# A two-layer transformer trunk: work moved off GpSimd, the feed-forward norm on ScalarE, other buffers for the down product's first loads

## The chip, the core and the metric

The kernel runs on one core of a Trainium2 chip. The metric is the device time of one execution in microseconds. Three runs of the kernel before gave a median of 2775.42 us (2772.57 to 2777.33). The engines are TensorE (PE, matmuls, with its weight loads as PEld), VectorE (DVE), ScalarE (ACT), GpSimd (POOL) and SyncE (SP), which issues the transfers.

## The reference, cut to what matters

The input is 1024 tokens of 1024 channels in fp32, and there are two layers. Each layer has a token mixer with two attention branches and a squared-relu feed-forward block:

```
h = rms_norm(x, mix_norm_g[l])
proj = h @ w_in[l]                      # q, k, v of both branches and two gates
o_sb  = stick_breaking_attention(...)   # branch A, 8 heads of 64
q = apply_rope(rms_norm(sw_q, q_norm_g[l]), cos, sin)
k = apply_rope(rms_norm(sw_k, k_norm_g[l]), cos, sin)
y_swa = sliding_window_sink_attention(q, k, v, sinks[l]) @ w_branch_swa[l]
merged = gates[0] * (o_sb @ w_branch_sb[l]) + gates[1] * y_swa
x = x + merged @ w_out[l]
h2 = rms_norm(x, mlp_norm_g[l])         # x * rsqrt(mean(x*x) + eps) * g
x = x + square(relu(h2 @ w_up[l])) @ w_down[l]
```

`w_up` is 1024 x 4096 and `w_down` 4096 x 1024.

## The kernel before, in words

Every fp32 product is made of three fast matmuls: each operand is split into a high part, made by an ACT cast, and a low part, a DVE subtract of the high part from the source (L332 and L335 for the mixer's weights, L1266 and L1269 for the feed-forward part). `three` (L346 to L348) issues high·high, high·low and low·high. So each weight tile passes DMA, ACT and DVE before PE can use it.

The order of the instructions is fixed when the program is built. A model of the machine, `Plan`, runs processes that ask for an engine ("A" ACT, "D" DVE, "G" GpSimd, "P" PE, "S" SP) with a cost and a rank, and each engine's queue gets its instructions in the order in which the model grants them. Each engine works its queue in that order, so an instruction that waits holds back all that stand behind it. SP's queue holds nearly all transfers. A change of a cost or of an engine thus changes the order of all queues a little.

A norm (`norm`, L413) handles one tile of 128 tokens: ACT squares and sums the row, `rsqrt_newton` (L350) makes y = rsqrt by Ln, Exp and one Newton step, DVE writes h = x·y·g in one 1024-column operation (L425), and PE transposes h in two groups of four 128-column blocks (L436). In the feed-forward norm ACT copies each group from PSUM into `kept` (L1376, `Quarters.store`).

The feed-forward products use a scheme of seven products for a 2x2 block product. In the up phase there are 16 pairs per layer, each of 84 matmuls, products in the order 1, 2, 6, 5, 3, 4, 7 by their operands. Products 6, 5, 3 and 4 need sums of weight blocks, which POOL makes from the two tiles of 128x1024 that a pair loads (`two("G", ...)`, L1283, four per pair: `s1`, `a21`, `a11`, `a12`). They also need sums of token quarters, made once per layer (`mixing`, L1280, L1354, `t`). Results are combined out of PSUM on DVE (L1583), squared after relu by one DVE operation (`relu2`, L1542), summed again and stored to a DRAM scratch `u_scr` (L1547).

The down phase loads two operands per step: stored activations `dr<-u_scr` (L1756) and weights `dr<-in_w_down_dram` (L1770). Their first buffers are those that the up phase used for raw, high (`wh`) and low (`wl`) weight tiles; `a_ring` and `b_ring` (L1672) list which buffer each load takes. A unit of the `wh`/`wl` ring comes free when the up phase is done with it.

In window attention GpSimd scales the gain table `gt` (L510), negates the sinks (L512) and makes the rotary table of each token tile, `tab` (L547, 128x640). The operand `st` of the attention (L662) is transposed on PE at L668.

Of the kernel before, what the change touches and what calls it, by code (L numbers as in the profile page):

```python
# [198 lines left out]
def tile_hybrid_trunk(ctx: ExitStack, tc: tile.TileContext, x, g_mix, g_mlp, g_rope, sinks, rope,  # L199
# [150 lines left out]
    def rsqrt_newton(sp, y, v, n):  # L350
        lnv = sp.tile([P, n], F32, tag="rs_l", name="rs_l", bufs=4)
        yield "A", .1
        act_set(LOGEXP)
        nc.scalar.activation(lnv, v, AF.Ln)
        yield "A", .1
        nc.scalar.activation(y, lnv, AF.Exp, scale=-0.5)
        a = sp.tile([P, n], F32, tag="rs_a", name="rs_a", bufs=4)
        yield "D", .12
        nc.vector.tensor_tensor(a, y, y, ALU.mult)
        yield "D", .12  # L360
        nc.vector.tensor_tensor(a, a, v, ALU.mult)
        yield "D", .12
# [98 lines left out]
    def load_g(npool, row, rank):  # L461
        ev = Event(plan)

        def go():
# [6 lines left out]
        plan.spawn(go(), rank)  # L471
        return ev
# [7 lines left out]
    def swa_phase(l, base, sw, swp, hT, normed, o_scr, tab_scr, finished, tail, projected):  # L480
# [15 lines left out]
        def consts(g):  # L496
# [14 lines left out]
            yield "G", .1  # L511
            nc.gpsimd.tensor_scalar(snk[:, 1], snk[:, 0], -1.0, None, ALU.mult)  # L512
# [18 lines left out]
        def tables(g, t):  # L531
# [14 lines left out]
            yield "G", gps(640)  # L546
            nc.gpsimd.tensor_tensor(tab, cev[g].value[0], rt.unsqueeze(2).broadcast_to([P, 2, 5, HD]), ALU.mult)  # L547
# [1118 lines left out]
    def down_phase(l, base, quads, u_scr, t_scr, u_ev, tail_raw, tail_ring, wide, late_on, x_ev, x3_ev, dst, saved, splits_done, finished):  # L1666
# [5 lines left out]
        a_ring = (("raw", None), ("raw", None), ("wl", 0), ("wl", 1), ("wh", 2), ("wh", 3))  # L1672
        b_ring = (("wh", 0), ("wh", 1), ("wl", 2), ("wl", 3)) + (("dr", None),) * 4 + (("late", None),) * LATE_RAWS
# [222 lines left out]
    def driver():  # L1896
# [4 lines left out]
        for l in range(depth):  # L1901
# [62 lines left out]
            g_ev = load_g(npool, g_mlp[l], base + 60510)  # L1964
# [3 lines left out]
            quads = Quarters(ep, base + 75000, normed)  # L1968
# [57 lines left out]
def _layout(inputs):  # L2026
# [25 lines left out]
    def swap(g):  # L2052
# [14 lines left out]
        "g_mlp": c(i["mlp_norm_g"].reshape(L, 1, D)),  # L2067
# [34 lines left out]
```

## Time and profile before

| What | Value |
|---|---|
| Median of three runs | 2775.42 us |
| The profiled execution | 2772.42 us, its span 2770.6 us |
| Mean granted TensorE clock | 0.994 |
| TensorE busy | 2708.4 us, 13568 matmuls |
| DVE busy | 1920.9 us |
| ACT busy | 1246.6 us |
| POOL busy | 221.1 us |

A row of a timeline gives the start, the length, the engine, the line, the operation, and in brackets how long the engine had been idle and what released it. A row of a group gives the count, the busy time, the mean length of one in ns, then idle time ahead. `PEclk` is the granted TensorE clock as a share of full speed.

### The profile page before, as it was taken

To read this page: it belongs to the slowest core of one execution; us is meant where nothing else is said; L and a number is where in the kernel's file an instruction comes from. 1 tells how busy PE (TensorE), PEld (TensorE's weight loads), DVE (VectorE), ACT (ScalarE), POOL (GpSimd) and SP (SyncE) were. 2 spreads that over 40 slices of the span, in tenths; PEclk is the share of its full clock that TensorE was granted. 3 is DMA by queue.
4 is the path that set the end of the run, shared out by engine and by line. 5 is a ranking of instruction groups with operands and counts; after the bars stand their busy time and mean duration, and the time that the engine had idled before them with its cause. 6 is when DMAs were issued, how large, how long until landed. Compare 5 with 4: busy or idle time off the path is not lost. (4 is left out here: it accounts for less than half of the span.)

```text
span 2770.6 us, 37073 instructions
## 1 busy us (share of the span) xinstructions
PE 2708.4 (98%) x13568; PEld 2281.4 (82%) x13568; DVE 1920.9 (69%) x3247; ACT 1246.6 (45%) x2521; POOL 221.1 (8%) x233
## 2 busy tenths in 40 slices
PE   7999999999989999999999999999999999999999
PEld 6888888888868877888888888888887777778887
DVE  6665888765587677767666658887547867678664
ACT  5776566642432223333457765565425222234332
POOL 1000000000032221000010000000000322200000
PEclk9999999999999999999999999999999999999999
DMA  5232222264124347996333222123530445389972
GB/s 171 81 92 62 61 62 58 68 225 157 31 103 167 132 161 270 354 370 244 137 116 99 71 62 65 50 64 126 180 135 32 144 127 166 126 314 354 342 265 92
DMA packets 159382, 411.00 MB, mean 148 GB/s; under 512 B 18656, under 2 KB 32992, under 8 KB 159200
## 3 DMA queue, kind: packets, MB, share of 16 engines
q1 hardware_dynamic: 159200, 408.63, 42.9%
q8 instruction: 107, 1.75, 0.3%
q14 instruction: 75, 0.61, 0.1%
HBM read 285.88 MB, written 114.29 MB: 144 GB/s over the span
## 5 line engine op out<-in xcount | busy, mean ns | idle before, releaser
L1266 ACT CAST operand<-dr 128x1024 fp32r<-128x1024 f32 x224 | 220.1, 1049 | 369.7 <-PE bank L348 173.7
L346 PE MATMUL bank<-operand 128*128 128x512 f32 x896 | 350.3, 391 | 5.8 <-ACT operand L1266 5.8
L347 PE MATMUL bank<-operand 128*128 128x512 f32 x896 | 350.5, 391 | 3.0 <-DVE operand L1269 3.0
L348 PE MATMUL bank<-operand 128*128 128x512 f32 x896 | 349.7, 390 | 0.0
L1269 DVE TENSOR_TENSOR operand<-dr,operand 128x1024 fp32r<-128x1024 f32 x224 | 262.7, 1218 | 121.0 <-ACT operand L1266 117.9
L346 PE MATMUL bank<-hT,wh 128*128 128x512 f32 (+1 forms) x776 | 312.4, 403 | 0.0
L348 PE MATMUL bank<-hT,wl 128*128 128x512 f32 (+1 forms) x776 | 302.9, 390 | 0.0
L347 PE MATMUL bank<-hT,wh 128*128 128x512 f32 (+1 forms) x776 | 302.2, 389 | 0.0
L1266 ACT CAST wh<-raw 128x512 fp32r<-128x512 f32 x128 | 79.4, 621 | 442.2 <-POOL raw L1283 254.7
L1269 DVE TENSOR_TENSOR wh<-raw,wh 128x512 fp32r<-128x512 f32 x128 | 102.5, 801 | 146.7 <-ACT wh L1266 146.7
L346 PEld LDWEIGHTS bank<-operand 128*128 128x128 f32 x896 | 168.8, 188 | 42.8 <-ACT operand L1266 7.5
L347 PEld LDWEIGHTS bank<-operand 128*128 128x128 f32 x896 | 168.9, 189 | 39.0 <-DVE operand L1269 4.3
L348 PEld LDWEIGHTS bank<-operand 128*128 128x128 f32 x896 | 169.0, 189 | 35.0
L348 PEld LDWEIGHTS bank<-hT,wl 128*128 128x128 f32 x776 | 146.3, 189 | 31.6
L347 PEld LDWEIGHTS bank<-hT,wh 128*128 128x128 f32 x776 | 147.1, 190 | 23.3
L346 PEld LDWEIGHTS bank<-hT,wh 128*128 128x128 f32 x776 | 147.3, 190 | 22.9
L335 DVE TENSOR_TENSOR wl<-raw,wh 128x1024 fp32r<-128x1024 f32 x88 | 107.0, 1219 | 57.5 <-ACT wh L332 56.8
L332 ACT CAST wh<-raw 128x1024 fp32r<-128x1024 f32 x88 | 92.2, 1050 | 106.6 <-PE bank L348 76.6
L1283 POOL TENSOR_TENSOR stage<-raw 128x512 f32<-128x512 f32 x32 | 53.0, 1657 | 863.1 <-ACT kept L1376 437.9
L999 DVE TENSOR_TENSOR_SCAN keep<-keep 128x128 f32<-128x128 f32 (+3 forms) x128 | 100.0, 808 | 16.2 <-ACT keep L988 16.2
L1058 DVE TENSOR_TENSOR tl<-bank,th 128x512 fp32r<-128x512 f32 (+1 forms) x160 | 97.6, 626 | 17.9 <-ACT th L1056 16.2
L988 ACT ACTIVATE keep<-bank 128x128 f32<-128x128 f32 (+1 forms) x192 | 91.3, 499 | 38.9 <-PE bank L982 23.4
(199 smaller groups left out, 6676.0 us busy)
## 6 DMA issues: line engine op xcount, KB each, us to landing
dr<-in_w_down_dram SPq DMA_DIRECT2D x144, 512.0 KB, 8.1
dr<-u_scr SPq DMA_DIRECT2D x112, 512.0 KB, 7.5
u_scr<-up SPq DMA_DIRECT2D x160, 256.0 KB, 4.4
raw<-in_w_up_dram SPq DMA_DIRECT2D x68, 512.0 KB, 4.3
raw<-in_w_gate_dram SPq DMA_DIRECT2D x32, 512.0 KB, 4.2
g_scr<-stage SPq DMA_DIRECT2D x64, 256.0 KB, 2.4
gate<-g_scr SPq DMA_DIRECT2D x64, 256.0 KB, 3.0
u_scr<-stage SPq DMA_DIRECT2D x64, 256.0 KB, 3.7
```

The lines of the kernel that those rows point to most:

```text
L332: nc.scalar.copy(hi[:, :n], raw[:, :n])
L335: nc.vector.tensor_tensor(lo[:, :n], raw[:, :n], f32(hi[:, :n]), ALU.subtract)
L346: nc.tensor.matmul(ps_ap, ah, bh, start=first, stop=False)
L347: nc.tensor.matmul(ps_ap, ah, bl, start=False, stop=False)
L348: nc.tensor.matmul(ps_ap, al, bh, start=False, stop=last)
L988: nc.scalar.activation(keep[:, lo:512], z, AF.Sigmoid, scale=-1.0)
L999: nc.vector.tensor_tensor_scan(later[:, ::-1], later[:, ::-1], later[:, ::-1], ini, ALU.mult, ALU.bypass)
L1058: nc.vector.tensor_tensor(tl[:, :n], tr[:, :n], f32(th[:, :n]), ALU.subtract)
L1266: nc.scalar.copy(op.hi(j, n), src)
L1269: nc.vector.tensor_tensor(op.lo(j, n), src, f32(op.hi(j, n)), ALU.subtract)
L1283: nc.gpsimd.tensor_tensor(out, a, b, op)
```

## The change

1. `rsqrt_newton` takes the sum of squares itself: Ln gets the scale 1/D and eps as bias, ACT also squares y, and three small DVE operations are left of five.
2. In the feed-forward norm ACT writes h = x·y (a Copy with y as scale), without the gain. The gain, loaded as one value per channel row ([128, 8]), is applied in the copies out of PSUM, where one 512-column ACT copy becomes four scaled 128-column ones. The mixer's norm keeps its DVE operation.
3. `gt`, `snk` and `tab` are made on DVE, and so are the four sums of weight blocks per pair.
4. The squared relu is two ACT operations, Relu and Square.
5. The two rings of buffers for the down phase's first loads are listed differently.

```diff
-    def rsqrt_newton(sp, y, v, n):
+    def rsqrt_newton(sp, y, ss):
...
-        nc.scalar.activation(lnv, v, AF.Ln)
+        nc.scalar.activation(lnv, ss, AF.Ln, scale=1.0 / D, bias=eps_t)
         nc.scalar.activation(y, lnv, AF.Exp, scale=-0.5)
+        nc.scalar.activation(a, y, AF.Square)
...
-        nc.vector.tensor_tensor(a, y, y, ALU.mult)
+        nc.vector.scalar_tensor_tensor(a, ss, D * EPS, a, ALU.add, ALU.mult)
...
-        nc.vector.tensor_tensor(a, a, v, ALU.mult)
-        nc.vector.tensor_scalar(a, a, -0.5, 1.5, ALU.mult, ALU.add)
+        nc.vector.tensor_scalar(a, a, -0.5 / D, 1.5, ALU.mult, ALU.add)
...
     def norm(...):
-        nc.vector.tensor_scalar(v, ss, 1.0 / D, EPS, ALU.mult, ALU.add)
-        yield from rsqrt_newton(npool, y, v, 1)
-        yield g_ev
-        yield "D", dve(D)
-        nc.vector.scalar_tensor_tensor(h, xt, y, g_ev.value, ALU.mult, ALU.mult)
+        yield from rsqrt_newton(npool, y, ss)
+        if dst.gains:
+            yield "A", act(D)
+            nc.scalar.activation(h, xt, AF.Copy, scale=y)
+        else:
+            yield g_ev
+            yield "D", dve(D)
+            nc.vector.scalar_tensor_tensor(h, xt, y, g_ev.value, ALU.mult, ALU.mult)
...
     consts, tables:
-                yield "G", gps(512)
-                nc.gpsimd.tensor_scalar(gt[:, :, 0:4], gt[:, :, 0:4], -0.125, None, ALU.mult)
+                yield "D", dve(512)
+                nc.vector.tensor_scalar(gt[:, :, 0:4], gt[:, :, 0:4], -0.125, None, ALU.mult)
...
-            yield "G", gps(640)
-            nc.gpsimd.tensor_tensor(tab, cev[g].value[0], rt..., ALU.mult)
+            yield "D", dve(640)
+            nc.vector.tensor_tensor(tab, cev[g].value[0], rt..., ALU.mult)
...
     Quarters.store:
-            yield "A", act(512)
-            nc.scalar.copy(self.kept[half, kh][:, :, q * P:(q + 1) * P], pt)
+            yield self.g_ev
+            yield "A", 4 * act(128)
+            for k in range(4):
+                nc.scalar.activation(self.kept[half, kh][:, k, q * P:(q + 1) * P], pt[:, k], AF.Copy,
+                                     scale=self.g_ev.value[:, 4 * kh + k:4 * kh + k + 1])
...
     operands (up phase):
-            yield from two("G", s1, a21, a22, ALU.add)
-            yield from two("G", a21, a11, a21, ALU.subtract)
-            yield from two("G", a11, s1, a11, ALU.subtract)
+            yield from two("D", s1, a21, a22, ALU.add)
+            yield from two("D", a21, a11, a21, ALU.subtract)
+            yield from two("D", a11, s1, a11, ALU.subtract)
...
-                yield from two("G", a12, a12, a11, ALU.subtract)
+                yield from two("D", a12, a12, a11, ALU.subtract)
...
             def relu2(t):
-                yield "D", dve(512)
-                nc.vector.scalar_tensor_tensor(t, t, 0.0, t, ALU.max, ALU.mult)
+                yield "A", 2 * act(512)
+                nc.scalar.activation(t, t, AF.Relu)
+                nc.scalar.activation(t, t, AF.Square)
...
     down_phase:
-        a_ring = (("raw", None), ("raw", None), ("wl", 0), ("wl", 1), ("wh", 2), ("wh", 3))
-        b_ring = (("wh", 0), ("wh", 1), ("wl", 2), ("wl", 3)) + (("dr", None),) * 4 + (("late", None),) * LATE_RAWS
+        a_ring = (("raw", None), ("raw", None), ("wh", 2), ("wl", 2), ("wh", 3), ("wl", 3))
+        b_ring = (("wh", 0), ("wl", 0), ("wh", 1), ("wl", 1)) + (("dr", None),) * 4 + (("late", None),) * LATE_RAWS
```

The orders of the queues move with it. On DVE, in the loop over pairs of the first layer, the rows around the seventh product read before (`wh` and `wl` are splits of weights, `bank` a result in PSUM, `up` and `stage` partial results):

```order
L1280 TENSOR_TENSOR stage<-stage,up 128x512
L1269 TENSOR_TENSOR wl<-raw,wl 128x512
L1583 TENSOR_TENSOR stage<-bank,stage 128x512
L1269 TENSOR_TENSOR wh<-raw,wh 128x512
L1583 TENSOR_TENSOR up<-bank,stage 128x512
L1269 TENSOR_TENSOR wh<-raw,wh 128x512
L1269 TENSOR_TENSOR wl<-raw,wl 128x512
L1583 TENSOR_TENSOR up<-bank,up 128x512
L1542 SCALAR_TENSOR_TENSOR up<-up 128x512
```

and in the changed kernel, where the lines of L1269, L1280 and L1583 are L1278, L1289 and L1598:

```order
L1289 TENSOR_TENSOR stage<-stage,up 128x512
L1598 TENSOR_TENSOR stage<-bank,stage 128x512
L1278 TENSOR_TENSOR wl<-raw,wl 128x512
L1289 TENSOR_TENSOR stage<-raw 128x512
L1289 TENSOR_TENSOR raw<-raw 128x512
L1598 TENSOR_TENSOR up<-bank,stage 128x512
L1289 TENSOR_TENSOR raw<-stage,raw 128x512
L1289 TENSOR_TENSOR raw<-raw 128x512
L1278 TENSOR_TENSOR wh<-raw,wh 128x512
L1598 TENSOR_TENSOR up<-bank,up 128x512
L1278 TENSOR_TENSOR wl<-stage,wl 128x512
```

The four sums of L1289 (`stage<-raw`, `raw<-raw`, `raw<-stage,raw`, `raw<-raw`) stand among the splits and evictions, the squared relu (L1542) is gone from DVE.

On SP, at the first layer's passage from the up to the down phase, before:

```order
L1547 DMA u_scr_7288<-stage 128x512
L1547 DMA u_scr_7288<-up 128x512
L1756 DMA dr<-u_scr_7288 128x1024
L1547 DMA u_scr_7288<-up 128x512 x4
L1547 DMA u_scr_7288<-stage 128x512
L1770 DMA dr<-in_w_down_dram 128x1024
L1756 DMA dr<-u_scr_7288 128x1024 x3
L1770 DMA dr<-in_w_down_dram 128x1024
```

and in the changed kernel (L1547, L1756 and L1770 are L1562, L1771 and L1785):

```order
L1771 DMA dr<-u_scr_7272 128x1024 x2
L1562 DMA u_scr_7272<-stage 128x512
L1562 DMA u_scr_7272<-up 128x512
L1785 DMA dr<-in_w_down_dram 128x1024
L1562 DMA u_scr_7272<-up 128x512
L1785 DMA dr<-in_w_down_dram 128x1024
L1562 DMA u_scr_7272<-up 128x512 x3
L1562 DMA u_scr_7272<-stage 128x512
L1785 DMA dr<-in_w_down_dram 128x1024 x2
L1771 DMA dr<-u_scr_7272 128x1024 x6
```

The first weight of the down product stands two stores behind the first loads of activations, and the second one a store later; before, the first stood behind all these stores.

On ACT, at the last tile of the first feed-forward norm, before (`xt` is a token tile, `t` a sum of quarters):

```order
L417 ACTIVATE h,ss<-xt_7276 128x1024
L1589 COPY stage<-bank 128x512
L354 ACTIVATE rs_l<-v 128x1
L356 ACTIVATE y<-rs_l 128x1
L1376 COPY kept<-bank 128x4x128 x2
L1354 CAST t_7283<-stage 128x4x128
L1589 COPY stage<-bank 128x512
L1376 COPY kept<-bank 128x4x128 x2
```

and in the changed kernel (L417, L1376, L1354 and L1589 are L418, L1389, L1365 and L1604):

```order
L418 ACTIVATE h,ss<-xt_7260 128x1024
L1389 ACTIVATE kept<-bank,g 128x128 x8
L356 ACTIVATE rs_l<-ss,eps_t 128x1
L357 ACTIVATE y<-rs_l 128x1
L358 ACTIVATE rs_a<-y 128x1
L1604 COPY stage<-bank 128x512
L1365 CAST t_7267<-stage 128x4x128
L423 ACTIVATE h<-xt_7260,y 128x1024
L1389 ACTIVATE kept<-bank,g 128x128 x8
```

Eight scaled pieces stand where two copies did, and the scaled copy of the tile (L423) is ACT's.

## Rows read from the trace of the kernel before

**Rows 1.** the page's part 1: engine, busy us (share) and instructions.

```profile
PE 2708.4 (98%) x13568; PEld 2281.4 (82%) x13568; DVE 1920.9 (69%) x3247; ACT 1246.6 (45%) x2521; POOL 221.1 (8%) x233
```

**Rows 2.** table of windows: from:to, length, busy us of each engine, PEclk, DMA share, GB/s.

```profile
0.00:100.00 100.00, 80.92 (x454) 72.33 (x455) 64.95 (x170) 58.99 (x160) 15.49 (x20) 0.97 0.42 141
700.00:815.00 115.00, 106.23 (x479) 85.98 (x478) 85.84 (x151) 54.05 (x107) 23.36 (x12) 0.97 0.19 63
1063.00:1095.00 32.00, 27.39 (x110) 21.29 (x110) 27.36 (x37) 12.19 (x14) 0.00 (x0) 0.95 0.88 324
1400.00:1470.00 70.00, 65.27 (x357) 58.16 (x355) 42.05 (x110) 38.65 (x109) 15.56 (x10) 0.98 0.38 124
2085.00:2187.00 102.00, 93.25 (x421) 75.15 (x420) 81.77 (x146) 49.45 (x103) 23.08 (x12) 0.97 0.18 62
2442.00:2470.00 28.00, 23.75 (x95) 18.40 (x95) 23.69 (x33) 10.42 (x12) 0.00 (x0) 0.94 0.89 332
```

**Rows 3.** PE's waits: what for, us in total, times, longest.

```profile
PE bank L668 <- DVE st L662: 9.4, 4, 5.0
PE bank L346 <- ACT wh L1266: 8.0, 4, 3.5
```

**Rows 4.** table of windows, 3.3 us behind the passage's gaps.

```profile
1079.40:1082.70 3.30, 3.29 (x8) 2.62 (x9) 2.31 (x3) 2.47 (x3) 0.00 (x0) 0.50 1.03 418
```

**Rows 5.** timeline of PE (start us, us, operation): starts of pairs in the up loop.

```profile
812.94 0.39 PE L346 MATMUL bank<-t,wh 128*128 128x512 f32 x1
...
1063.04 0.39 PE L346 MATMUL bank<-t,wh 128*128 128x512 f32 x1
...
2184.68 0.39 PE L346 MATMUL bank<-t,wh 128*128 128x512 f32 x1
...
2185.36 0.39 PE L346 MATMUL bank<-t,wh 128*128 128x512 f32 x1
...
2440.53 0.41 PE L346 MATMUL bank<-t,wh 128*128 128x512 f32 x1
```

**Rows 6.** timelines of DVE, PE and POOL in the up loop, then one group of DVE.

```profile
2340.66 1.24 DVE L1269 TENSOR_TENSOR wh<-raw,wh 128x512 fp32r<-128x512 f32 x1 [5.86 <-ACT wh L1266]
...
2341.96 0.50 PE L348 MATMUL bank<-t,wh 128*128 128x512 f32 x1 [0.54 <-DVE wh L1269]
...
781.44 6.53 POOL L1283 TENSOR_TENSOR stage<-raw 128x512 f32<-128x512 f32 x1 [15.03 <-DVE up L1583]
...
L1269 DVE TENSOR_TENSOR wl<-raw,wl 128x512 fp32r<-128x512 f32 x64 | 43.7, 682 | 0.0
```

**Rows 7.** groups of DVE (operation, count, busy us, mean ns): the squared relu.

```profile
L1542 DVE SCALAR_TENSOR_TENSOR up<-up 128x512 f32<-128x512 f32 x96 | 68.5, 714 | 1.0
```

**Rows 8.** timeline of ACT: quarters copied out of PSUM, two tiles of a norm.

```profile
716.56 1.07 ACT L1376 COPY kept<-bank 128x512 f32<-128x512 f32 x2 [2.83 <-PE bank L436]
...
722.92 1.07 ACT L1376 COPY kept<-bank 128x512 f32<-128x512 f32 x2 [3.58 <-PE bank L436]
```

**Rows 9.** groups of ACT: an operation with a scale from memory.

```profile
L741 ACT ACTIVATE pr<-pr,sm 128x128 f32<-128x128 f32 x16 | 5.1, 389 | 1.5 <-DVE sm L736 0.8 <-DVE a L614 0.7
```

**Rows 10.** timelines of DVE and PE at layer 1's start, then one group of DVE.

```profile
1428.41 1.24 DVE L614 SCALAR_TENSOR_TENSOR a<-v,a 128x5 f32<-128x5 f32 x1 [0.32 <-ACT a L612]
...
1431.09 0.72 PE L668 MATMUL bank<-ident_r,st 128*128 128x128 f32 x4 [3.35 <-DVE st L662]
...
L614 DVE SCALAR_TENSOR_TENSOR a<-v,a 128x5 f32<-128x5 f32 x32 | 7.3, 228 | 10.6 <-ACT a L612 10.6
```

**Rows 11.** timelines of SP, ACT and PE at the passage to the down product.

```profile
1071.71 0.59 SPq L1770 DMA_DIRECT2D dr<-in_w_down_dram  x1
...
1077.05 1.04 ACT L1266 CAST operand<-dr 128x1024 fp32r<-128x1024 f32 x1 [3.91 <-DMA dr<-in_w_down_dram]
...
1078.14 0.49 PE L346 MATMUL bank<-operand 128*128 128x512 f32 x1 [1.26 <-ACT operand L1266]
...
1079.40 0.80 PE L347 MATMUL bank<-operand 128*128 128x512 f32 x1 [0.77 <-DVE operand L1269]
```

More of the change, by code (lines that the diff above doesn't have):

```diff
@@ L348, in three @@
         nc.tensor.matmul(ps_ap, al, bh, start=False, stop=last)
-    def rsqrt_newton(sp, y, v, n):
-        lnv = sp.tile([P, n], F32, tag="rs_l", name="rs_l", bufs=4)
-        yield "A", .1
+    def rsqrt_newton(sp, y, ss):
+        lnv = sp.tile([P, 1], F32, tag="rs_l", name="rs_l", bufs=4)
+        a = sp.tile([P, 1], F32, tag="rs_a", name="rs_a", bufs=4)
+        yield "A", .45
         act_set(LOGEXP)
-        nc.scalar.activation(lnv, v, AF.Ln)
-        yield "A", .1
+        nc.scalar.activation(lnv, ss, AF.Ln, scale=1.0 / D, bias=eps_t)
         nc.scalar.activation(y, lnv, AF.Exp, scale=-0.5)
-        a = sp.tile([P, n], F32, tag="rs_a", name="rs_a", bufs=4)
+        nc.scalar.activation(a, y, AF.Square)
         yield "D", .12
-        nc.vector.tensor_tensor(a, y, y, ALU.mult)
+        nc.vector.scalar_tensor_tensor(a, ss, D * EPS, a, ALU.add, ALU.mult)
         yield "D", .12
-        nc.vector.tensor_tensor(a, a, v, ALU.mult)
-        yield "D", .12
-        nc.vector.tensor_scalar(a, a, -0.5, 1.5, ALU.mult, ALU.add)
+        nc.vector.tensor_scalar(a, a, -0.5 / D, 1.5, ALU.mult, ALU.add)
         yield "D", .12
@@ L386, in tile_hybrid_trunk @@
     class Halves(list):
+        gains = False
         def open(self, half):
@@ L459, in open_x, with load_g, columns @@
         return xp
-    def load_g(npool, row, rank):
+    def load_g(npool, row, rank, col=False):
         ev = Event(plan)
+        def columns():
+            yield "S", .45
+            g_c = npool.tile([P, NK], F32, tag="g", name="g")
+            nc.sync.dma_start(out=g_c, in_=row)
+            yield moved(NK * 512)
+            ev.set(g_c)
         def go():
@@ L469, in go @@
             ev.set(g_bc)
-        plan.spawn(go(), rank)
+        plan.spawn(columns() if col else go(), rank)
         return ev
@@ L508, in consts @@
             if g == 0:
-                yield "G", gps(512)
-                nc.gpsimd.tensor_scalar(gt[:, :, 0:4], gt[:, :, 0:4], -0.125, None, ALU.mult)
-            yield "G", .1
-            nc.gpsimd.tensor_scalar(snk[:, 1], snk[:, 0], -1.0, None, ALU.mult)
+                yield "D", dve(512)
+                nc.vector.tensor_scalar(gt[:, :, 0:4], gt[:, :, 0:4], -0.125, None, ALU.mult)
+            yield "D", .12
+            nc.vector.tensor_scalar(snk[:, 1], snk[:, 0], -1.0, None, ALU.mult)
             cev[g].set((gt, snk))
@@ L545, in tables @@
             yield moved(128 * 512)
-            yield "G", gps(640)
-            nc.gpsimd.tensor_tensor(tab, cev[g].value[0], rt.unsqueeze(2).broadcast_to([P, 2, 5, HD]), ALU.mult)
+            yield "D", dve(640)
+            nc.vector.tensor_tensor(tab, cev[g].value[0], rt.unsqueeze(2).broadcast_to([P, 2, 5, HD]), ALU.mult)
             use = Shared(2, tab_s.release)
@@ L1293, in tile_hybrid_trunk, with __init__ @@
     class Quarters:
-        def __init__(self, ep, rank, normed):
-            self.ep, self.rank = ep, rank
+        gains = True
+        def __init__(self, ep, rank, normed, g_ev):
+            self.ep, self.rank, self.g_ev = ep, rank, g_ev
             self.ops = {"6": wide_operand(ep.tile([P, NK, 512], F32R, name="t2"), 16, lambda: None)}
@@ L1963, in driver @@
             npool = pool("norm", side="right")
-            g_ev = load_g(npool, g_mlp[l], base + 60510)
+            g_ev = load_g(npool, g_mlp[l], base + 60510, True)
             ep = pool("up")
@@ L1967, in driver @@
             normed = [Event(plan, 2) for _ in range(NT)]
-            quads = Quarters(ep, base + 75000, normed)
+            quads = Quarters(ep, base + 75000, normed, g_ev)
             used = Event(plan, NT)
@@ L2066, in _layout @@
         "g_mix": c(i["mix_norm_g"].reshape(L, 1, D)),
-        "g_mlp": c(i["mlp_norm_g"].reshape(L, 1, D)),
+        "g_mlp": c(i["mlp_norm_g"].reshape(L, NK, P).transpose(0, 2, 1)),
         "g_rope": c(g_rope),
```

2 lines of the change are left out of this document (removed).

## The prediction, made before the changed kernel ran

> **What bounds the kernel now.** I read the page's busy shares first. TensorE is busy 2708.4 of 2770.6 us, DVE 69%, ACT 45%, POOL 8% [rows 1]. The change leaves the 13568 matmuls as they are, so what can be won is TensorE's idle time, about 62 us, and what its clock costs. A table of the span by windows then tells where the idle time lies: window length less PE busy is 19.1 us in the first 100, 8.8 where the first feed-forward norm is made (700 to 815), 4.6 around the passage from the up to the down product (1063 to 1095), 4.7 at the start of layer 1 (1400 to 1470), 8.75 and 4.25 at the same places of layer 1 [rows 2]. The reader should see that no engine's total matters here: a few places do. PE's list of waits names who was late: 9.4 us, the longest 5.0, for the window-attention operand `st`, 8.0 for ACT's cast `wh` of a weight [rows 3].
>
> A gap of some 2 us costs more than itself: the 3.3 us behind the gaps of the passage show a granted clock of 0.50, that is 1.2 instead of 2.4 GHz, and 8 matmuls where 14 or 15 fit [rows 4]. Such a stretch is about 3.4 us long, so each costs 1.7. The clock column of the windows [rows 2] tells how many there are: 0.97 over 115 us is two stretches, 0.95 over 32 and 0.98 over 70 one each.
>
> The up loop does not show as idle time but as period. Three matmuls take 2185.36 − 2184.68 = 0.68 us, so the 84 of a pair take 19.04. Thirteen pairs take 250.10 us in layer 0 and 255.85 in layer 1 [rows 5], against 247.5: 2.6 and 8.35 us too long.
>
> **The change part by part.**
>
> *Weight mixing from POOL to DVE (128 operations).* Before, DVE's subtract of a weight takes 0.68 us as a rule, and 1.24 when a POOL operation runs beside it; PE then waits 0.54 for it, once in most pairs. Where DVE stays busy, POOL is the victim: one addition took 6.53 us at 781.44 [rows 6]. With the mixing on DVE nothing runs on POOL there, and the chain landing → four sums → cast is 4 × 0.68 on a queue that has some slack: DVE at 69% [rows 1] would be busy 13 of a pair's 19 us, and the change keeps that level, since 4 sums per pair come and 4 squared relus go. In the new order all four sums stand right behind the seventh product's work, a product ahead of the cast that needs them. I count the whole excess as gone: +11.0 (2.6 + 8.4). Bounds 0, if the wait only changes its cause, and 11.
>
> *Squared relu from one DVE operation to two ACT operations.* DVE loses 128 × 0.71 us, 96 of the row's form and 32 like it [rows 7]; ACT gains 256 × 0.54, by two 512-column copies in 1.07 us [rows 8], 4.3 us per pair. ACT does casts and little else in the up loop, so I count 0. Without that cover a cast stands behind two relus, 1.07 us per pair, 34 us in all 32 pairs; less than 0 is excluded since nothing on PE waits for the old operation. The Trainium skill, page "ScalarE: Activation LUTs", section "Rules for kernel authors", speaks against this edit: it puts relu, max and multiplications on VectorE, not ScalarE. The rows agree that DVE does in one pass what ACT does in two, but the rule counts cost on the engine and not on the path; a late ACT is the second rival below.
>
> *Feed-forward norm on ACT, gain in the copies out of PSUM.* Per token tile ACT before copies two quarters in 1.07 us, and PE's pace per tile is 722.92 − 716.56 = 6.36 us [rows 8]. Now it makes a scaled copy of the tile (twice 0.54) and eight pieces of 128 columns. A 128x128 operation with a scale from memory takes 5.1/16 = 0.32 us [rows 9], so the eight are 2.55: 1.5 more per tile, plus 1.07 for `h`, which leaves DVE. With the square (about 1.2, a 1024-column pass like `h`), three small ACT steps, the wait for three small DVE steps and their handing over (1.3 together, an estimate by hand), ACT's round is about 6.4 us against PE's 6.36: a first half that just keeps up, and a second half, where casts and product copies are also due, in which tiles 5 to 7 each come 1 to 1.3 us late. My placement by hand gives gaps of 9.1 us and one half-clock stretch (1.7), 10.8; before there are 8.8 and two stretches (3.4), 12.2, of which the slow POOL addition caused a good part. So +1 per layer, +2 in all, bounds −4 and +8 (a gap more or less of 2 us with its clock, in each layer).
>
> *Shorter Newton step, gains of the mixer's norm unchanged.* Two small DVE operations go per tile and a small one on ACT comes; only the first tile of the kernel, of all mixer norms, has PE waiting long for it. I count 0, bounds ±1.
>
> *Rotary tables from POOL to DVE.* The 16 products of 640 columns, about 0.9 us each by columns from the 512-column subtract, now stand in DVE's queue, with a wait on a DMA. Behind them wait the casts' subtracts and the norm of q and k. I take −2 (two places, a DMA's microsecond each), bounds 0 and −6. At the start of layer 0 the `st` gap of 5.0 gains about 0.5: POOL no longer works beside that chain.
>
> *Start of layer 1.* PE waits 3.35 us for `st` at 1431.09. On that chain a DVE operation of 5 columns took 1.24 us, where the mean of its kind is 0.23 [rows 10]; it ran beside a POOL table product. That is 1.0 of the gap. Ahead of the chain stood two subtracts of gate weights, each waiting for a weight's landing and cast; in the new order one of them comes later, which by the 1024-column subtract gives 1.2 and with the wait for its cast an estimated 1.6. So 2.6 of the gap goes, and with it the half clock: +4.3, bounds 0 and 5.
>
> *Other buffers for the second product's first loads.* Before, the first down weight is issued at 1071.71, behind five stores of the last products; the cast starts as it lands, at 1077.05, and PE, done with the pair, begins at 1078.14 after 1.26 us and waits again, 0.77, at 1079.40 [rows 11]. In the new order two weights stand between the stores. I put the first landing at about 1068.4 (its buffer is free when the last pair's second product ends, 1063.04, where its third begins [rows 5]; and 5.3 for the transfer, as 1071.71 to 1077.0 shows), 8 us ahead of need. So the idle 4.6 + 4.25 of the two windows [rows 2] goes, and a half-clock stretch with each, 1.7: 12.2, bounds 0 and 12.2, since nothing more is idle there.
>
> **Sum.** 11.0 + 0 + 2 + 0 − 2 + 0.5 + 4.3 + 12.2 = 28.0. The profiled execution took 2772.42 us, 1.8 around its span, which gives 2744.4; the median of the runs shown is 3.0 higher, so I predict 2747 us.
>
> **Rivals.**
> 1. *The passages stay.* Stores and loads share SP's queue and the 16 DMA engines (share 0.88 in that window [rows 2]), so an earlier issue may land no earlier. Against it: a transfer issued 5 us sooner is worked on sooner. 2747 + 12 = 2759.
> 2. *The up loop gets a new late engine.* ACT's two relus, or DVE's four sums waiting for a weight's landing with products' evictions queued behind them, hold back as much as POOL did: the 11 us stay, 2758. If the relus hold a cast in every pair (34 us), it is 2747 + 34 = 2781. For it: in-order queues with a wait added. Against: PE has 12 products' worth of operands standing by, and the new order puts sums and casts a product early.
> 3. *Slower: the norm's ACT round sets the pace.* The place is the eight tiles of each feed-forward norm. With 1.5 + 1.07 us more ACT work per tile, sixteen tiles cost up to 41 us where none is hidden; I hide most. From 28/16 = 1.75 us per tile on, what the rest gives back is eaten; with gaps long enough for the half clock (four more stretches per layer, 14 us) 2747 + 24 + 14 = 2785. Against it: PE has other products' matmuls to put between the tiles.
> 4. *Nothing arrives*: gaps only change their cause, 2770 to 2775.
>
> **How the numbers follow.** Forecast 0.62 (its own range 2739 to 2755, from the bounds of ramps and tables); the passages stay 0.15; the up loop's 11 us stay 0.08; nothing 0.05; relus in every cast 0.04; the norm's pace 0.06. A measurement tells 0.2%, some 5.5 us, from no change. Faster is 0.62 + 0.15 + 0.08 = 0.85, same 0.05 and the better half of the relu case and some of the mixed ones, 0.08, slower 0.07. The range for 8 in 10 runs from 2734, where ramps gain their upper bound, to 2767, where the passages stay and the ramps lose.
>
> **What would show it.** Up loop: pairs of 19.04 us and no wait of PE for `wh`. Passages: the first down weight lands before the last pair is done, and no half clock is seen there. Layer 1: the gap for `st` under 1 us. Norm: gaps of about 1 us for tiles 5 to 7, released by ACT's `kept` or `h`. It is wrong if PE's idle time in the two norm windows rises above 12 us each, or pairs stay above 19.5.

## The result, and the profile after

The changed kernel takes 2730.48 us (median of 4 runs, 2729.47 to 2733.76), the kernel before beside it 2776.33 (2772.57 to 2777.33). The ratio is 0.9839, interval 0.9822 to 0.9856. The forecast was 2747, in a range of 2734 to 2767: the direction is right, the gain was 45.9 us instead of 28, and the time lies below the range.

Of the profiled execution, the page's busy times and then windows at the places of [rows 2], shifted by what had been won so far:

```profile
PE 2691.5 (99%) x13568; PEld 2274.0 (83%) x13568; DVE 1879.6 (69%) x3189; ACT 1445.3 (53%) x2921; POOL 8.8 (0%) x83
```

```profile
0.00:100.00 100.00, 80.90 (x461) 72.71 (x462) 63.95 (x167) 63.62 (x172) 1.87 (x11) 0.98 0.41 141
700.00:810.00 110.00, 104.72 (x480) 82.98 (x479) 72.35 (x133) 82.33 (x188) 0.00 (x0) 1.00 0.18 65
1055.00:1090.00 35.00, 35.00 (x156) 29.00 (x155) 27.44 (x30) 20.10 (x24) 0.00 (x0) 1.00 1.01 382
1385.00:1455.00 70.00, 67.64 (x376) 60.22 (x375) 42.51 (x121) 43.48 (x123) 0.00 (x0) 1.00 0.38 124
2066.00:2163.00 97.00, 91.75 (x422) 72.28 (x421) 68.61 (x128) 78.25 (x183) 0.00 (x0) 1.00 0.19 67
2407.00:2435.00 28.00, 28.00 (x125) 23.17 (x125) 23.48 (x27) 18.58 (x23) 0.00 (x0) 1.00 1.03 376
```

Both passages are without idle time and at full clock. The norm stretches are idle for 5.3 us where they were for 8.8 [rows 2], and the clock no longer falls there. What PE waits for now (compare [rows 3]):

```profile
PE bank L438 <- DVE h L427: 15.9, 4, 10.8
PE bank L438 <- ACT h L423: 5.1, 8, 1.1
PE bank L677 <- DVE a L623: 3.1, 1, 3.1
PE bank L347 <- DVE taken L1278: 3.0, 4, 1.2
PE bank L677 <- DVE st L671: 2.4, 1, 2.4
PE bank L346 <- ACT wh L1275: 1.0, 2, 0.5
```

A better account than idle time comes from PE itself: the matmuls are the same in both kernels, so the start of the same one (the k-th of its operands) can be compared. The starts of pairs that answer to [rows 5], on PE's timeline:

```profile
807.48 0.39 PE L346 MATMUL bank<-t,wh 128*128 128x512 f32 x1
...
1055.00 0.39 PE L346 MATMUL bank<-t,wh 128*128 128x512 f32 x1
...
2159.31 0.39 PE L346 MATMUL bank<-t,wh 128*128 128x512 f32 x1
...
2406.83 0.39 PE L346 MATMUL bank<-t,wh 128*128 128x512 f32 x1
```

Thirteen pairs take 247.5 us in both layers. By such landmarks 41.4 of the 41.7 us between the two profiled executions fall to stages as in the first row of this table. "Start to norm" runs from the start of the kernel, or the end of layer 0's down product, to the first transposes of the feed-forward norm. "Norm" runs on to the first matmul of a layer in [rows 5], so the first two pairs are in it. "Up loop" is the thirteen pairs, and "passage" runs from there to a matmul of the down product behind its last wait. The other rows are the experiments below, each against the profile of before; the last columns are the sum of the stages and the ratio with its interval. Negative is won. The down products are left out: they differ by 0.1 us at most in every kernel.

| Kernel | start to norm, layer 0 | norm | up loop | passage | start to norm, layer 1 | norm | up loop | passage | all | ratio (interval) |
|---|---|---|---|---|---|---|---|---|---|---|
| changed | −0.3 | −5.2 | −2.6 | −7.4 | −4.7 | −5.2 | −8.3 | −7.7 | −41.4 | 0.984 (0.982, 0.986) |
| o_mix | 1.0 | −3.6 | −2.6 | −7.2 | −0.4 | −4.9 | −8.3 | −7.2 | −33.3 | 0.986 (0.985, 0.988) |
| o_tab | −3.1 | 0.8 | −0.9 | 0.8 | −6.6 | 0.6 | 2.1 | 2.1 | −4.3 | 0.996 (0.995, 0.998) |
| o_pool | −1.9 | −3.7 | −2.6 | −7.4 | −7.1 | −4.9 | −8.3 | −7.7 | −43.6 | 0.982 (0.981, 0.983) |
| o_rings | 1.7 | 0.0 | 1.2 | −2.9 | 1.2 | 0.6 | 1.6 | −1.0 | 2.5 | 0.999 (0.998, 1.000) |
| x_plan | 3.4 | −0.6 | −2.6 | −7.4 | −0.3 | −1.2 | −8.3 | −7.4 | −24.3 | 0.988 (0.987, 0.990) |
| x_exec | 3.5 | −5.4 | −2.6 | −3.3 | 1.5 | −5.4 | −8.3 | −6.0 | −26.1 | 0.987 (0.985, 0.988) |
| u_mix | −0.3 | 5.3 | −2.6 | −5.0 | −3.6 | 5.1 | −8.3 | −3.6 | −13.1 | 0.993 (0.991, 0.995) |
| u_tab | 5.3 | −5.2 | −2.6 | −7.4 | −1.8 | −5.2 | −8.3 | −7.7 | −32.8 | 0.987 (0.986, 0.989) |
| u_rings | −1.9 | −5.2 | −2.6 | −6.3 | −6.2 | −5.2 | −8.3 | −7.2 | −42.8 | 0.983 (0.981, 0.985) |
| u_norm | 1.4 | −7.2 | −2.6 | −7.4 | −3.4 | −7.1 | −8.3 | −7.7 | −42.4 | 0.982 (0.980, 0.983) |
| u_gain | −1.6 | −8.3 | −2.6 | −7.4 | −6.1 | −8.3 | −8.3 | −7.7 | −50.2 | 0.980 (0.979, 0.982) |
| u_relu | 1.0 | −4.7 | −2.6 | −7.4 | −3.5 | −3.1 | −8.3 | −7.7 | −36.3 | 0.984 (0.982, 0.986) |
| u_newton2 | 0.3 | −6.4 | −2.6 | −7.4 | −7.3 | −6.3 | −8.3 | −7.7 | −45.7 | 0.980 (0.978, 0.982) |
| v_gd | −2.2 | −6.3 | −2.6 | −7.4 | −6.2 | −6.3 | −8.3 | −7.7 | −46.9 | 0.982 (0.980, 0.983) |
| v_gd_r | 1.8 | −4.7 | −2.6 | −7.3 | −3.4 | −6.3 | −8.3 | −7.3 | −38.1 | 0.983 (0.982, 0.985) |

How far the columns repeat differs. The two "start" columns carry noise of up to 3.5 us: o_mix, x_plan, x_exec and o_rings change nothing ahead of layer 0's norm and differ from before by 1.0 to 3.5 there. The norm columns repeat to 0.1 us as long as the clock does the same: u_norm and another execution of the same kernel (u_newton) agree to 0.1 in layer 0, and in layer 1, where the clock fell to half for 3.4 us in the second alone, they differ by 1.4. The up loops of the old order drift by up to 2.1 (o_tab, o_rings), and so do o_tab's passages, though these edits lie elsewhere; a loop without waits repeats to 0.1.

One profile stands for each kernel, and it need not be a middling one. The profile of before, 2772.42 us, is 4 to 6.6 us faster than the medians that the ratios use (2776.33 to 2778.99), so the stages add up to less than the medians differ. The profile of x_exec, 2746.47, is 5.5 us slower than its median.

### The profile page after: what moved, and what is told of

It is laid out like the page before. It is cut to its first block, busy times and chain, and to the rows that moved or that the text cites. A ratio compares the mean times of both kernels' runs of the same rounds, so it can differ in the third digit from the quotient of the medians.

```text
span 2728.9 us, 37192 instructions
## 1 busy us (share of the span) xinstructions
PE 2691.5 (99%) x13568; PEld 2274.0 (83%) x13568; DVE 1879.6 (69%) x3189; ACT 1445.3 (53%) x2921; POOL 8.8 (0%) x83
## 4 chain that ended last, share of the span: by engine, by line
PE 91%; ACT 4%; DVE 3%; DMA 1%; issue 1%; SPq 0%; ACTq 0%; DVEq 0%
PE bank L346 27%; PE bank L348 26%; PE bank L347 26%; PE bank L1059 2%; PE bank L988 1%; PE bank L1092 1%; PE bank L1091 1%; PE bank L989 1%; PE bank L703 1%; PE bank L770 1%; ACT kept L1389 1%; PE bank L438 1%; ACT h L418 1%; PE bank L793 0%; DVE pr L712 0%
## 5 line engine op out<-in xcount | busy, mean ns | idle before, releaser
L1278 DVE TENSOR_TENSOR operand<-dr,operand 128x1024 fp32r<-128x1024 f32 x224 | 263.2, 1222 | 117.0 <-ACT operand L1275 117.0
L1065 ACT CAST th<-bank 128x512 fp32r<-128x512 f32 (+1 forms) x160 | 83.3, 546 | 51.8 <-PE bank L1059 48.6
L1289 DVE TENSOR_TENSOR dr<-dr 128x1024 f32<-128x1024 f32 x64 | 78.1, 1224 | 44.2 <-DMA dr<-t_scr 22.8
```

Source lines behind the costliest of these rows:

```text
L1065: nc.scalar.copy(th[:, :n], tr[:, :n])
L1278: nc.vector.tensor_tensor(op.lo(j, n), src, f32(op.hi(j, n)), ALU.subtract)
L1289: nc.vector.tensor_tensor(out, a, b, op)
```

## The experiments

Kernels u_… are the changed one with a part undone, o_… the kernel before with a part put in, x_… split one part in two, v_… apply the gain in another way.

**u_mix: the sums of weight blocks back on POOL.**

```diff
-            yield from two("D", s1, a21, a22, ALU.add)      # and the three other sums
+            yield from two("G", s1, a21, a22, ALU.add)
```

> The changed kernel (2730.5 us) with the four sums of weight blocks per pair back on POOL, all else as changed. Theory P (POOL beside DVE was the cost, in the up loops and in the feed-forward norm too): thirteen pairs take 250 and 256 us again (+2.6 and +8.4), and the two norm stretches lose most of the 5.2 us that each gained, since the long POOL addition, the gap of 3.5 behind it and its half-clock stretch come back: about 2751. Rival N (the norm stretches gained because h left DVE): only the up loops lose, 2741.5.

2759.7 us, 9 more than theory P said. In the norm stretches it holds and falls short: they lose 10.5 and 10.3 us against the changed kernel. The first two of the four sums ahead of the first pair on POOL, PE's wait, the clock behind it, and SP's first down weight:

```profile
763.19 1.49 POOL L1292 TENSOR_TENSOR stage<-raw 128x512 f32<-128x512 f32 x1 [223.06 <-DMA raw<-in_w_up_dram]
764.75 1.63 POOL L1292 TENSOR_TENSOR raw<-raw 128x512 f32<-128x512 f32 x1
```

```profile
773.12 0.50 PE L346 MATMUL bank<-t,wh 128*128 128x512 f32 x1 [3.30 <-ACT wh L1275]
```

```profile
773.80:780.60 6.80, 6.05 (x15) 4.75 (x15) 6.80 (x13) 6.80 (x14) 0.00 (x0) 0.50 0.18 58
```

```profile
1070.88 1.15 SPq L1785 DMA_DIRECT2D dr<-in_w_down_dram  x2
```

But both theories miss the up loops, which stay at 19.04 us per pair although POOL works there, and the passages, which lose 2.4 and 4.1.

**u_norm: the feed-forward norm as before.**

```diff
-        if dst.gains:
-            nc.scalar.activation(h, xt, AF.Copy, scale=y)
+        nc.vector.scalar_tensor_tensor(h, xt, y, g_ev.value, ALU.mult, ALU.mult)
...
-            for k in range(4):                      # scaled pieces, Quarters.store
+            nc.scalar.copy(self.kept[half, kh][:, :, q * P:(q + 1) * P], pt)
```

> The changed kernel with the feed-forward norm as before: h and gain in one DVE operation, one 512-column copy per quarter on ACT; POOL stays empty. Theory P: the norm stretches lose nothing, since DVE without POOL beside it makes h in 1.28 us; ACT's round no longer sets a pace of 6.51 us per tile, so 2726 to 2732. Rival N: both stretches lose their 5.2 us, 2741.

2727.35 us: theory P. The old norm is 2.0 us faster in each stretch, so the new one is a cost that the rest covers. Another execution of the same kernel (u_newton) took 2727.68; there the old norm is 2.1 us faster in layer 0 and 0.7 in layer 1, where the clock fell once.

**u_gain: the gain left out, one copy instead of four.**

```diff
-            for k in range(4):
-                nc.scalar.activation(kept..., pt[:, k], AF.Copy, scale=...)
+            nc.scalar.copy(self.kept[half, kh][:, :, q * P:(q + 1) * P], pt)
```

> The changed kernel with the gain of the feed-forward norm left out: one unscaled 512-column copy out of PSUM instead of four scaled 128-column ones. Theory A (ACT's round sets the pace of the norm): a tile's period falls from 6.51 to 6.36 us and the gaps of 0.58, 0.65 and 0.25 us for h go: 2.3 us per layer, 2726. Rival (the tiles wait for something else, DVE's y or the residual): the same within 1 us, 2730.

This kernel leaves out the gain, so it prices that part and computes something else. 2723.98 us, 3.05 us less per norm stretch, where theory A said 2.3: theory A. ACT's copies come 6.36 us apart, as in [rows 8]:

```profile
714.97 1.08 ACT L1388 COPY kept<-bank 128x512 f32<-128x512 f32 x2 [0.75 <-PE bank L438]
...
721.33 1.07 ACT L1388 COPY kept<-bank 128x512 f32<-128x512 f32 x2 [0.80 <-PE bank L438]
```

**u_rings and o_rings: the rings alone, taken out and put in.**

```diff
-        a_ring = (("raw", None), ("raw", None), ("wh", 2), ("wl", 2), ("wh", 3), ("wl", 3))
+        a_ring = (("raw", None), ("raw", None), ("wl", 0), ("wl", 1), ("wh", 2), ("wh", 3))
...                                                                  # and b_ring; o_rings the other way
```

> The changed kernel with the two buffer rings listed as before. Theory R (the rings move the first down loads ahead of the stores): both passages lose their gaps and a half-clock stretch again, 7.4 and 7.65 us: 2745.5. Rival (the loads came early because the rest of the queue order changed, with the sums and relus elsewhere): 2731.

> The kernel before with only the two buffer rings listed as in the changed kernel. Theory R: the passages give 15 us, 2761. Rival (the stores of the last pair, late because of POOL, still stand ahead of the loads): less than half of that, 2769 or more.

u_rings 2732.13, o_rings 2774.31 against 2778.98 (ratio 0.9976 to 0.9995). Theory R falls, and both rivals hold. Without the new rings the passages lose only 1.1 and 0.5, and alone they give 2.9 and 1.0. SP's first down weight in u_rings, and in o_rings (compare 1071.71 in [rows 11]):

```profile
1054.99 0.58 SPq L1785 DMA_DIRECT2D dr<-in_w_down_dram  x1
```

```profile
1074.25 1.29 SPq L1770 DMA_DIRECT2D dr<-in_w_down_dram  x2
```

In u_rings the load is issued 16.7 us sooner than in before, but 9.7 of these had been won ahead of it. Against PE's own work, the landmark in the last pair (1063.04 in before), SP issues it 8.7 us behind in before, 8.4 in o_rings, 1.6 in u_rings, and 0.3 us ahead of it in the changed kernel. So something other than the rings brings the load forward by 7 us, and the rings by 1.9 more.

**u_relu: the squared relu on DVE.**

```diff
-                nc.scalar.activation(t, t, AF.Relu)
-                nc.scalar.activation(t, t, AF.Square)
+                nc.vector.scalar_tensor_tensor(t, t, 0.0, t, ALU.max, ALU.mult)
```

> The changed kernel with the squared relu back as one DVE operation. Theory (the edit only moves covered work): all pairs stay at 19.04 us, 2730 within 2 us. Rival (DVE would be too full with sums and relus, 2.9 us more per pair, and late with subtracts): pairs lengthen by 0.5 us or more, 16 us in all, 2746. Second rival (the rule that relu belongs on DVE): ACT gets free, 2 to 5 us less in the norm stretches, 2726.

2733.56 us, 1.6 above what the theory allowed, pairs at 19.04. In the loops the edit moves covered work. In the norm stretches PE is idle 0.9 us longer in each layer, and in layer 1 the clock also falls for 3.4 us, which together make the 2 us of that column. Neither rival holds.

**u_tab and o_tab: the rotary tables, taken back to POOL and moved alone.**

```diff
-            nc.vector.tensor_tensor(tab, cev[g].value[0], ..., ALU.mult)     # and gt, snk
+            nc.gpsimd.tensor_tensor(tab, cev[g].value[0], ..., ALU.mult)
```

> The changed kernel with the rotary tables, the gain table and the sinks' negation back on POOL. Theory P: DVE operations at the window attention's start run beside POOL again; layer 1's start loses the 1.0 us of the slowed 5-column operation and perhaps its half-clock stretch, 1.7: 2731 to 2734. Rival (my prediction's term: DVE's queue is held by the tables' landings): POOL takes that wait away again, 2728.

> The kernel before with only the rotary tables, the gain table and the sinks' negation moved to DVE. Undoing this part in the changed kernel cost 5.5 us up to the first feed-forward norm and 3 at layer 1's start. Theory (tables beside DVE slow the first attention's chains): the mirror, 5 to 8 us less, 2771. Rival (the loss there came from the order of the queues with the shorter Newton step, not from POOL): within 2 us, 2778. My prediction's own term said 2 us more, 2780.

u_tab 2742.26 (12 us lost, more than either theory said), o_tab 2768.84 (10 us won, more than its theory's 5 to 8). The profiles of o_tab and before differ by 4.3 only: the two starts give 9.7, and the other stages drift the other way. In u_tab 5.6 and 2.9 us are lost ahead of the two norms, at the first attentions above all: in u_tab PE waits 5.02 for the first `st` again, in the changed kernel 3.11 at the same place:

```profile
62.76 0.72 PE L677 MATMUL bank<-ident_r,st 128*128 128x128 f32 x4 [5.02 <-DVE a L623]
```

```profile
60.69 0.72 PE L677 MATMUL bank<-ident_r,st 128*128 128x128 f32 x4 [3.11 <-DVE a L623]
```

**o_mix: the sums alone on DVE, in the kernel before.**

```diff
-            yield from two("G", s1, a21, a22, ALU.add)      # and the three other sums
+            yield from two("D", s1, a21, a22, ALU.add)
```

> The kernel before (2776 us) with only the four sums of weight blocks per pair moved to DVE. Theory P: the up loops give 11 us and the norm stretches several us each, in all 15 to 20: 2756 to 2761. Rival (DVE with sums and relus is too full): the loops keep their excess or get worse, 2770 to 2790.

2739.72 us. One part alone gives 39 us, the passages too, with the old rings. That was twice what theory P said, so I split it.

**x_plan and x_exec: the order and the engine apart.** In x_plan the sums stay on POOL and are planned as DVE's; in x_exec they run on DVE and are planned as POOL's.

```diff
+    def mixed(out, a, b, op, n=512):
+        yield "D", dve(n)                       # x_exec: "G", gps(n)
+        nc.gpsimd.tensor_tensor(out, a, b, op)  # x_exec: nc.vector
```

> The kernel before (2778 us in these runs) with the four sums still on POOL, but with all queues ordered as if they were DVE operations (cost 0.60 instead of 1.40 in the model). It separates the order from the engine, after the sums alone on DVE gave 39 us. Theory O (the order: the raw fetches run one pair further ahead, so the first down loads are issued some 13 us earlier): the passages give their 13 us and the up loops 11, about 2752. Theory E (the engine: a POOL sum takes 1.3 us and more beside DVE): nothing or a loss, since the chains planned at 0.60 take twice that, 2775 to 2795.

> The kernel before with the four sums run on DVE, but all queues ordered as if they still took POOL's 1.40 us. Theory E: each sum takes 0.6 to 0.7 us without a partner that slows it, so the up loops give 11 us and the norm stretches 4 to 5 each, and the passages stay as they are, since the first down loads are issued at the same place of SP's queue: about 2758. Theory O: the fetch order is as before, so the loops and passages stay, and only the norm stretches gain: 2768 to 2772.

2746.43 and 2740.98. The split is clean: by the traces SP, PE and ACT work through the same order in x_exec as in before, and in x_plan as in o_mix. x_plan does what theory O says and 5 us more, x_exec does 17 more than theory E says, so neither holds alone. The up loops are cured by either. The passages are the order's (14.8 us of x_plan's gain), the engine alone gives 9.3. The norm stretches are the engine's: 5.4 each, against 0.6 and 1.2 by the order. A sum takes 1.46 us on POOL in x_plan and 0.69 on DVE in x_exec, and a subtract beside it 0.84 against 0.69:

```profile
L1287 POOL TENSOR_TENSOR raw<-raw 128x512 f32<-128x512 f32 x64 | 93.6, 1463 | 17.3 <-DVE wl L1269 13.8
```

```profile
L1269 DVE TENSOR_TENSOR wh<-raw,wh 128x512 fp32r<-128x512 f32 x128 | 107.7, 842 | 36.5 <-ACT wh L1266 36.5
```

```profile
L1287 DVE TENSOR_TENSOR raw<-raw 128x512 f32<-128x512 f32 x64 | 44.0, 687 | 0.9
...
L1269 DVE TENSOR_TENSOR wh<-raw,wh 128x512 fp32r<-128x512 f32 x128 | 87.7, 685 | 4.9 <-ACT wh L1266 3.9
```

**o_pool: sums and tables on DVE, nothing else.** The edits of o_mix and o_tab together.

> The kernel before (2778 us) with both moves from POOL to DVE together (sums and tables), but the old norm, Newton step, relu and rings. Alone they gave 39 and 10 us. Theory P (leaving POOL is all of it): they add up, 2729 to 2733, as fast as the changed kernel. Rival (the other parts carry a share of the norm stretches and the passages): 2738 or more, by the 33.3 and 4.3 us that the stages of the two profiles show.

2728.31 us, ratio 0.9819 (0.9805 to 0.9834): theory P. The two moves off POOL, with the order that they bring, are the whole gain; norm, relu, Newton step and rings together give nothing that these runs can tell.

**u_newton2: the old Newton step in the changed kernel.**

```diff
+        nc.vector.tensor_scalar(v, ss, 1.0 / D, EPS, ALU.mult, ALU.add)
...
-        nc.scalar.activation(a, y, AF.Square)
-        nc.vector.scalar_tensor_tensor(a, ss, D * EPS, a, ALU.add, ALU.mult)
+        nc.vector.tensor_tensor(a, y, y, ALU.mult)
+        nc.vector.tensor_tensor(a, a, v, ALU.mult)
```

> The changed kernel with the old Newton step (five small DVE operations instead of three, one ACT operation less). Theory (only the first tiles of the mixer's norm wait on it, and there DVE's h waits for the gain): the same within 2 us, 2730. Rival (the step is on ACT's and DVE's round of each feed-forward tile): 0.2 us per tile, 3 us in all, 2733.

2723.09 us, ratio 0.9800 (0.9784 to 0.9816): faster than the changed kernel by 7, and the fastest version tried that computes everything; its interval lies just below the changed kernel's (0.9822 to 0.9856). Both theories miss the sign. The shorter step puts a Square on ACT, whose round sets the norm's pace: 1.1 us per stretch, and PE's waits for ACT's `h` fall from 5.1 to 0.9 us in all. At the start of the kernel PE waited 15.9 us for DVE's `h` with the new step; with the old one the first two of these lines stand in its place, and the third is the wait for ACT:

```profile
PE bank L442 <- DVE rs_a L359: 10.6, 1, 10.6
...
PE bank L442 <- DVE h L431: 2.4, 2, 2.0
...
PE bank L442 <- ACT h L427: 0.9, 4, 0.3
```

At the start that is 2.9 us less idle time, though the half-clock stretch at the first attention was longer in that execution (10.2 us instead of 3.4), which hides it in the table. The edit also changes what the plan counts for the step, so work and order are not told apart here.

**v_gd and v_gd_r: the gain as a DVE multiplication out of PSUM, with the new and the old rings.**

```diff
-            for k in range(4):
-                nc.scalar.activation(kept..., pt[:, k], AF.Copy, scale=...)
+            nc.vector.tensor_tensor(kept..., pt, g[:, 4 * kh:4 * kh + 4] repeated along tokens, ALU.mult)
```

> The changed kernel (2730.5 us) with the gain applied by one DVE multiplication out of PSUM per quarter (the gain column repeated along the tokens, planned at 0.3 us) instead of four scaled ACT copies. Leaving the gain out gave 3 us per layer in the norm stretches. Theory A (ACT's round is the pace): ACT gets 2.0 us per tile back and DVE has room, so nearly the same is won: 2724 to 2726. Rival: DVE, which in these stretches is busy 77 of 115 us, gets late with y or with evictions: 2730 or more.

> The changed kernel with the gain applied by one DVE multiplication per quarter, and the old rings. Theory (the rings matter little once the sums are on DVE, and the gain on DVE saves 1 us per norm stretch): 2727 to 2729. Rival (the rings' 1.6 us add): 2730.

2728.47 and 2732.40: 1 us won per norm stretch with the new rings, theory A in direction, less than half of u_gain's 3.05, and the time lies between theory A and the rival. With the old rings one stretch loses it again, to a half-clock stretch of 3.4 us, and the time lies above both theory and rival. Their intervals overlap the changed kernel's, so neither is shown to differ from it.

## Why the prediction was wrong in size, step by step

*The norm stretches, predicted +1 each, measured 5.2 each: the step that failed.* "My placement by hand gives gaps of 9.1 us and one half-clock stretch." Measured are gaps of 5.3 us and no half-clock stretch; the two layers gave 10.4, more than the upper bound of 8. The rows of ACT and PE in the changed kernel, layer 0:

```profile
716.31 2.17 ACT L1389 ACTIVATE kept<-bank,g 128x128 f32<-128x128 f32 x8 [0.75 <-PE bank L438]
```

```profile
750.67 0.77 PE L438 MATMUL bank<-ident,h 128*128 128x128 f32 x5 [0.58 <-ACT h L423]
...
757.19 0.98 PE L438 MATMUL bank<-ident,h 128*128 128x128 f32 x7 [0.65 <-ACT h L423]
...
764.02 1.09 PE L438 MATMUL bank<-ident,h 128*128 128x128 f32 x8 [0.25 <-ACT h L423]
...
780.90 0.50 PE L347 MATMUL bank<-taken,wl 128*128 128x512 f32 x1 [1.24 <-DVE taken L1278]
...
785.17 0.50 PE L346 MATMUL bank<-t,wh 128*128 128x512 f32 x1 [0.52 <-ACT wh L1275]
```

The eight pieces take 2.17 us, not the 2.55 of my neighbour row. Tiles 5 to 7 are late by 0.58, 0.65 and 0.25 instead of 1 to 1.3, no gap is over 1.3 us, and the clock stays full, where I had put one stretch. The mechanism of the third rival is real: u_gain and u_norm price ACT's part at 3.05 and 2.0 us per stretch, and beside a POOL that sums (u_mix) the new norm ends 5 us behind before.

On the other side I credited POOL's slow additions too little. These are the two long waits of PE in layer 0's stretch before, and then the stretch in before and in x_exec, which only takes the additions off POOL:

```profile
765.44 1.94 PE L436 MATMUL bank<-ident,h 128*128 128x128 f32 x8 [2.24 <-DVE h L425]
...
791.35 0.50 PE L346 MATMUL bank<-t,wh 128*128 128x512 f32 x1 [3.51 <-ACT wh L1266]
```

```profile
715.40:812.94 97.54, 88.77 (x402) 71.81 (x401) 77.83 (x138) 48.91 (x100) 23.36 (x12) 0.97 0.17 57
```

```profile
718.90:810.98 92.08, 87.77 (x401) 71.53 (x401) 77.67 (x150) 48.43 (x100) 0.00 (x0) 0.96 0.18 61
```

x_exec gives 5.4 in each layer. PE's idle time falls from 8.8 to 4.3 us: both waits go, and one of 2.1 for ACT's `t` comes. The half clock gives nothing there, since it lasts 6.8 us in both, as two stretches in before and one in x_exec. In the changed kernel the idle time falls less, by 3.5, but no half clock is left. Idle time and clock, 3.5 and 3.4, would give 6.9 a layer, and 5.2 arrived; where the rest went stays open. The two stretches are 8.4 us of the miss.

*The up loops, predicted 11.0, measured 10.9.* The size was right. The reason was one of two: x_plan shows that the order cures them too, with POOL still at 1.46 us per sum, and so does u_mix, where the relu left DVE. One reading was off: PE waits in 10 of the 26 pairs, not in most, and for 5.8 us in all. The size came out right because I took it from the period; the other half doesn't show as idle time, for the reason that follows.

*The passages, predicted 12.2, measured 15.0, by another cause than I gave.* I counted idle time and clock and bounded the term there, "since nothing more is idle". Half a microsecond is a wait of the last pair at 2441.72, ahead of my window. The other 2.2 don't show as idle time. A row of a matmul is 0.39 us long, though the next one starts after 0.227, so 0.16 of each gap counts as busy; and the first matmuls after a gap also stand further apart. In this stretch of the up loop of before, PE starts 0.94 us after the row ahead, of which 0.54 is idle [rows 6], and the next two follow the waiting one by 0.33 and 0.24:

```profile
2341.02 0.40 PE L347 MATMUL bank<-t,wh 128*128 128x512 f32 x1
...
2342.29 0.40 PE L346 MATMUL bank<-t,wh 128*128 128x512 f32 x1
2342.53 0.39 PE L347 MATMUL bank<-t,wh 128*128 128x512 f32 x1
```

And the load is early because of the sums, more than the rings. In layer 0, where they are planned on DVE (o_mix, x_plan and the changed kernel among others), SP issues the last up weight 22.9 us ahead of the landmark in the last pair, and 9.6 ahead of it in before and o_rings. The first down weight then follows 0.6 us behind that landmark with the old rings (o_mix, x_plan) and 0.3 us ahead of it in the changed kernel, instead of 8.7 behind. PE goes over without a gap:

```profile
1054.70 0.38 SPq L1785 DMA_DIRECT2D dr<-in_w_down_dram  x1
```

```profile
1068.37 0.39 PE L348 MATMUL bank<-taken,wh 128*128 128x512 f32 x1
1068.60 0.39 PE L346 MATMUL bank<-operand 128*128 128x512 f32 x1
```

I read the order of the changed kernel rightly, with the load 9.0 us sooner against PE's work where I had put 8.7, but put it down to the edit that names those buffers.

*Tables and layer 1's start, predicted 4.3 + 0.5 − 2, measured 5.0.* The −2 for DVE waiting on the tables' landings did not come; o_tab gains. The gap for `st` at layer 1 shrank by 1.0 only in this profile, not 2.6, but its half clock went, and most of the later small gaps of that attention too:

```profile
1412.43 0.54 PE L677 MATMUL bank<-ident_r,st 128*128 128x128 f32 x4 [2.35 <-DVE st L671]
```

It was 0.96 us in u_rings, where the changed kernel's queues differ at the passages alone, so the size of that gap varies between executions. With the noise of the start columns this miss of 2.2 us is not a clear one.

*Relu, counted 0:* right in the loops. *Newton step, counted 0, bounds ±1:* it costs 7 us by the medians of u_newton2, 4.3 by the profiles; ACT's round was at its limit and I looked at the first tile alone. *The base:* I took the median 3 us above the profiled execution for both kernels; the changed kernel's median is 0.2 below its own. The miss of 16.5 us is 8.4 + 2.8 + 2.2 of stages and about 3 of base. With every part at the better end of its bounds the sum would have been 2737 us, so the bounds were too narrow, too, where I worked from idle time. Two of my sums were loose as well: by the bounds that I gave, my own range ends at 2757, not 2755, and the two cases named for the wide range come to 2741 and 2765.

*The rivals.* The first (passages stay) and fourth did not happen. The second (a new late engine in the loop) did not either: ACT with two relus and DVE with four sums keep 19.04. The third happened in part, as above: its extra work on ACT is real, and the rest of the change covered it.

## What to carry to other kernels

An engine that is 8% busy can be the cause of most waits, if it shares work with a busy one: price its operations by the slowest row beside busy neighbours, add the half clock behind the gap, and look which buffers it holds. Take the size of a loss from the starts of the same matmuls, not from idle time. Where a program orders all queues by a cost model, test an edit's engine and its order apart; a gain at a place may belong to an edit somewhere else. And look for the engine at the edge of its round before adding even a 0.2 us operation to it.

## What was unexpected of the hardware

The length of a half-clock stretch varies between executions for the same cause. At the first attention x_plan has the same queues as before, and a gap of 4.98 us for `st` where before has 5.04. The clock is at half for 3.4 us in before (from 65.7 on it is full) and for over 10 in x_plan; windows of before, then the gap and a window of x_plan:

```profile
62.20:65.50 3.30, 3.07 (x13) 3.10 (x14) 2.83 (x7) 1.37 (x5) 1.56 (x1) 0.50 0.17 65
65.70:72.30 6.60, 6.60 (x43) 5.91 (x42) 5.91 (x24) 5.00 (x21) 1.57 (x1) 1.00 0.16 50
```

```profile
63.10 0.72 PE L668 MATMUL bank<-ident_r,st 128*128 128x128 f32 x4 [4.98 <-DVE st L662]
```

```profile
62.70:72.80 10.10, 9.70 (x38) 9.04 (x38) 7.39 (x24) 5.14 (x20) 2.08 (x2) 0.50 0.19 66
```

And the clock need not fall at all. In the changed kernel it does behind the gap of 3.11 us there; in u_rings, with the same queues up to that place, the gap is 3.16 and the clock stays full. A window of the changed kernel, then the gap and a window of u_rings:

```profile
60.30:63.70 3.40, 3.01 (x13) 2.94 (x14) 3.26 (x11) 1.10 (x3) 0.00 (x0) 0.50 0.00 0
```

```profile
60.44 0.51 PE L677 MATMUL bank<-ident_r,st 128*128 128x128 f32 x4 [3.16 <-DVE a L623]
```

```profile
60.40:70.60 10.20, 10.16 (x61) 9.29 (x62) 8.38 (x31) 7.35 (x28) 0.00 (x0) 1.00 0.20 71
```

So the half clock behind one gap costs nothing, 1.7 us or up to 5 here. That is a part of what executions of one kernel differ by (x_exec took 2746.47 us at a mean granted clock of 0.993, and 2740.01 at 0.997); how large a part was not worked out. Why the length differs stays open. What exactly frees the raw tiles earlier on the chip was read from the order and the issue times, and wasn't tried by itself.
